# A backbone step's output projection in the shadow of a scan: transpositions in the scans' PSUM banks, input blocks split one at a time

## The chip, the core and the metric

The kernel runs on one core of a Trainium2 chip. The metric is the device time of one execution in microseconds (us), the median of several runs. The core has five engines with a queue each: TensorE (PE in the profile; its weight loads are PEld), VectorE (DVE), ScalarE (ACT), GpSimd (POOL) and SyncE (SP), which here issues nearly all transfers. Engines wait for one another through semaphores, and each takes its own instructions strictly in order. Matmuls write to PSUM, a small memory of eight banks, from which VectorE and ScalarE read.

## The reference

One layer of a hybrid backbone, for 128 context tokens and 512 latent tokens of width 2048, is computed as one batch of 640 columns:

```python
h = _rmsnorm(x, lp['norm1_g']) * (1.0 + sc1) + sh1
p = h @ lp['w_in']
o_a, s_fin = _rwkv7_bidir(shift_fn(p[..., :C_SHIFT], ...), s0, lp)   # scans, both directions, 16 heads of 64
o_b = _chunk_gmlp(jax.nn.gelu(p[..., C_SHIFT:]), lp)                 # gated MLP over chunks of 128 tokens
x = x + g1 * (jnp.concatenate([o_a, o_b], axis=-1) @ lp['w_out'])
h = _rmsnorm(x, lp['norm2_g']) * (1.0 + sc2) + sh2
ff = (silu(h @ lp['w_ffn_gate']) * (h @ lp['w_ffn_up'])) @ lp['w_ffn_down']
return x + g2 * ff, s_fin
```

Each head's scan is a recurrence over the tokens with a 64 x 64 state. Here it is done in chunks of 64 tokens: eight steps for the latent tokens and two for the context, in both directions.

## The kernel before, in words

The program goes through w_in, the scans, the rest of w_out, and the feed-forward layer. The change lies in the scans and at the seams on both sides of them (about 1060 to 1360 us of the profile).

**Precision.** A float32 matmul operand is split into a rounded high part and the rest (`hi` and `lo` for weights, `oh` and `ol` for inputs), and three matmuls replace one: hi·oh, hi·ol and lo·oh. The split of a 128 x 640 input block is a cast on ScalarE and a subtraction on VectorE.

**w_out's input** is 16 blocks `kb` of 128 rows, stored in DRAM as `d_o`: 0 to 7 from the scans (one of each pair of heads), 8 to 15 from the gated MLP, which are there before the scans begin. `o_load(kb)` loads one and splits it. Eight of them fit in SBUF, in the slots (kb + 4) % 8: blocks 8 to 11 share their slots with 0 to 3, and 12 to 15 with 4 to 7.

**The scans.** `recur(p)` is the recurrence of pair p, a generator that TensorE's order is woven from. A step has matmuls into `w_ps`, `u_ps` and `s_ps`; VectorE and ScalarE read them, and VectorE makes the next state `SN`, which the next step's `w_ps` needs. These, and `swap` at a scan's beginning and end, take turns in a ring of four PSUM banks, the pool `pws` (tag "ws"); `y_ps` has a bank of its own. A hop calls `next` twice on each pair under way; a step takes three hops, a pair begins each ten hops (`OFF`), and there are 10·7 + 29 = 99 hops. `join` (tile `pO`) and `gate` (tile `pmm`) finish a pair that has been scanned. They use the one bank of the pool `po` (tag "g"), which VectorE reads out (L1308 and L1318).

**Wide matmuls beside them.** `wout_b()` is a second generator: w_out's product with blocks 8 to 15. For q = 0 (blocks 8 to 11) and q = 1 (blocks 12 to 15) it goes through the 16 column blocks m of the output, with 24 wide matmuls each (`big`, 128 x 320; L1086 to L1088), in portions of three that cost 0.4 in the mixer's budget; a loaded block costs 1.0. In q = 0 it also loads x's columns and transposes them: `pxT` (L1343), four transpositions and then one, into the bank of `po`, from which ScalarE copies them to `x1T` (L1344). `add_out` then adds the product to x1T on VectorE. The mixer `m3` runs blocks 8 to 11 and the first FRONT = 4 column blocks before the scans. In the scans each hop gives it an equal share of what is left but for the last REST = 6 column blocks, and that comes to two portions, six wide matmuls, in most hops:

```python
                m3.run(max(0.0, m3.left - REST * 3.2) / (hops - hop))
```

**What sets the order.** TensorE's order in the scans is as written (`manual_schedule`). The other engines' order is made by a scheduler, which can move an instruction ahead of where the code has it as soon as it takes its inputs to be there. `split` (L171 to L173) is the load and the split of a block of weights.

Of the kernel before, what the change touches and what calls it, by code (L numbers as in the profile page):

```python
# [10 lines left out]
F32 = mybir.dt.float32  # L11
# [8 lines left out]
P = 128  # L20
# [38 lines left out]
FRONT = 4  # L59
# [30 lines left out]
def flow_step(ctx: ExitStack, tc, x_prompt, x_sample, state_rwkv, c, c_ctx, w_mod, b_mod,  # L90
# [18 lines left out]
    def tpool(**a):  # L109
        if a.get("space") != DRAM:  # L110
            a["reuse_waits"] = "tile"
        return tc.tile_pool(**a)
# [861 lines left out]
    g = 0  # L974
# [83 lines left out]
    pbig = obx.enter_context(tpool(name="pbig", bufs=2, space=PSUM))  # L1058
    o_hi, o_lo = {}, {}

    def o_load(kb, src=None):

        j = (kb + 4) % 8
        o_hi[kb], o_lo[kb] = (obp[j // 4].tile([P, T], F32R, tag=f"{n}{j}", name=n) for n in ("oh", "ol"))
        raw = o_lo[kb].bitcast(F32) if src is None else src
        if src is None:
            nc.sync.dma_start(raw, d_o[kb])
        S.copy(o_hi[kb], raw)
        V.tensor_sub(o_lo[kb], raw, o_hi[kb].bitcast(F32))

# [2 lines left out]
    def wout(m, q):  # L1073


        halves = [pbig.tile([P, HALF], F32, tag="big", name="big") for _ in range(2)]
        n = KB * q + m
        for k in range(n if n == 0 else n + 1, min(n + 2, 2 * KB)):
            r0, c0 = (8 + 4 * (k // KB)) * P, k % KB * P
            ahead[k] = split(w_out[0, r0:r0 + 4 * P, c0:c0 + P], 4)  # L1080
        hi, lo = ahead.pop(n)
        for hf in range(2):
            s = slice(HALF * hf, HALF * hf + HALF)
            for k in range(4):
                kb = 8 + 4 * q + k
                TE.matmul(halves[hf], hi[:, k, :], o_hi[kb][:, s], start=(k == 0), stop=False)  # L1086
                TE.matmul(halves[hf], hi[:, k, :], o_lo[kb][:, s], start=False, stop=False)
                TE.matmul(halves[hf], lo[:, k, :], o_hi[kb][:, s], start=False, stop=(k == 3))  # L1088
                yield 0.4
            add_out(m, halves, hf)  # L1090
# [11 lines left out]
    with ExitStack() as ph:  # L1102
        rw = ph.enter_context(tpool(name="rw", bufs=1))
        sm = ph.enter_context(tpool(name="sm", bufs=2))
        po = ph.enter_context(tpool(name="po", bufs=1, space=PSUM))
        pws = ph.enter_context(tpool(name="pws", bufs=4, space=PSUM))
# [21 lines left out]
        def load_next():  # L1128
            if todo:
                _, p, ctx_, step = todo.pop(0)  # L1130
                r = rw.tile([P, 2, REC], F32, tag="rec", name="rec", bufs=NREC)
                nc.sync.dma_start(r, d_S[p].rearrange("p d c f -> p (d c) f")[:, flip(seqs[ctx_][step])])
                recs[p, ctx_, step] = r
# [165 lines left out]
        def join(p, i):  # L1299

            u = U[p]
            a, b = HV[i]
            ps = po.tile([P, 5, CH], F32, tag="g", name="pO")
            for cc in range(a, b):
                for h in range(2):
                    TE.matmul(ps[hsl(h), cc - a, :], u.Y[1][hsl(h), cc, :], I2[hsl(h), :], start=True, stop=True)
            dst = v3(u.bv)[:, a:b, :]
            V.scalar_tensor_tensor(out=dst, in0=ps, scalar=prm[:, C_GW + p:C_GW + p + 1],  # L1308
                                   in1=dst, op0=ALU.mult, op1=ALU.add)
# [14 lines left out]
        def wout_b():  # L1324

            for q in range(2):
                for kb in range(8 + 4 * q, 12 + 4 * q):
                    o_load(kb)
                    yield 1.0
                for m in range(KB):  # L1330
                    if q == 0:
                        xc = x1T[m].rearrange("p (t n) -> p t n", n=P)
                        for t0, src in ((0, x_sample[0]), (NT - 1, x_prompt[0])):
                            n = src.shape[0] // P
                            nc.sync.dma_start(xc[:, t0:t0 + n, :],
                                              src[:, m * P:(m + 1) * P].rearrange("(q t) c -> t q c", t=P))
                    for k, c in enumerate(wout(m, q)):
                        yield c
                        if q == 0 and k in (0, 2):
                            t0, t1 = ((0, 4), (4, 5))[k // 2]  # L1340
                            ps = po.tile([P, 4, P], F32, tag="g", name="pxT")
                            for t in range(t0, t1):
                                TE.transpose(ps[:, t - t0, :], xc[:, t, :], ident)  # L1343
                            S.copy(xc[:, t0:t1, :], ps[:, 0:t1 - t0, :])  # L1344
# [11 lines left out]
        S.copy(gss[64:96, 2], gss[32:64, 2].bitcast(F32))  # L1356
        m3 = Mixer()
        m3.add(wout_b(), 8.0 + 16 * 6.4)
        m3.run(4.0 + FRONT * 3.2)
        for _ in range(NREC - 4):  # L1360
            load_next()
        act, nxt, after = [], 0, []
        hops = OFF * (NPAIR - 1) + 29
        with tc.manual_schedule(engines={mybir.EngineType.PE}):
            for hop in range(hops):
                if hop == OFF * nxt and nxt < NPAIR:
                    act.append((nxt, recur(nxt)))
                    nxt += 1
                for p, gen in act:
                    next(gen)  # L1370
                for job in list(after):
                    if job[0] < 0:
                        next(job[2], None)
                    elif job[0] in (LATE, LATE + 1):
                        join(job[1], job[0] - LATE)
                for p, gen in list(act):
                    if next(gen, 0) == 0:
                        act.remove((p, gen))
                        after.append([-7, p, norm(p)])
                for job in list(after):  # L1380
                    if job[0] in (LATE + 2, LATE + 3):
                        gate(job[1], job[0] - LATE - 2)
                    job[0] += 1
                    if job[0] > LATE + 3:
                        after.remove(job)
                m3.run(max(0.0, m3.left - REST * 3.2) / (hops - hop))
                for _ in range(owed[1]):
                    load_next()
                owed[:] = 0, owed[0]
                if hop == hops - 12:  # L1390
                    for kb in range(4):
                        o_load(kb)

            assert not act
            (_, p, gen), = after
            for _ in gen:
                pass
            for i, work in enumerate((lambda: join(p, 0), lambda: join(p, 1), lambda: gate(p, 0), lambda: gate(p, 1))):
                while m3.left > (4 - i) * 1.6 - 0.1:
                    m3.run(0.01)  # L1400
                work()
            m3.drain()
# [77 lines left out]
    with ExitStack() as ph:  # L1480
# [58 lines left out]
        for hf in range(2):  # L1539
            s = slice(HALF * hf, HALF * hf + HALF)  # L1540
            for m in range(KB):
                if hf or m >= AHEAD:
                    four_blocks(hf, m, 0)
                ps = four_blocks(hf, m, 1)
# [517 lines left out]
    later = []  # L2062
# [75 lines left out]
    for t in (3, 4, 0, 1, 2):  # L2138
        for h in (1, 0):
            out = fin.tile([P, 4, 256], F32, tag=f"out{h}", name="out")  # L2140
            src = acc[:, 4 * h:4 * h + 4, t * 256:(t + 1) * 256]
# [36 lines left out]
```

## Time and profile before

| | |
|---|---|
| time, median of 3 runs | 3168.68 us (3168.43 to 3176.81) |
| the profiled execution's own time | 3172.49 us |
| its span, first to last instruction | 3170.7 us |
| TensorE, VectorE, ScalarE, GpSimd busy | 96%, 74%, 47%, 39% of the span |
| the scans | about 1085 to 1325 us |

In the profile, `out<-in` names the tiles that an instruction writes and reads, L1198 its line, and xN how many. In rows in order of time the first number is the start, the second the time taken, and brackets tell how long the engine sat idle before and what ended that. In a list of waits stand the total, the number of times, and the longest. In a table of stretches each engine has its busy time and the number of its instructions; then come the granted clock of TensorE as a share of full speed, the share of time in which the transfer engines were busy, and what they moved. SPq is SyncE's queue issuing a transfer.

### The profile page before, as it was taken

Reading aid. Unit: us, or ns where it says so; the run is one execution under the profiler, and the core shown is the slowest. Engines: PE = TensorE matmul, PEld = TensorE weight load, DVE = VectorE, ACT = ScalarE, POOL = GpSimd, SP = SyncE. Lnnn points to the kernel's source line nnn. Section 1 sums busy time; section 2 is a strip of 40 time slices with the busy share of each in tenths; the row PEclk is TensorE's granted clock in tenths of the full one; section 3 lists DMA queues with packets and bytes.
Section 4 is the critical chain, followed back from the end, with each engine's and each line's share of the span. In section 5 each row is a group of like instructions: output and inputs, shape, how many; then the busy total and the mean of one; then the engine's idle time right before and its main releaser. Section 6 shows DMA issues by size and latency. Waiting matters only on the chain.

```text
span 3170.7 us, 71552 instructions
## 1 busy us (share of the span) xinstructions
PE 3052.5 (96%) x27896; PEld 2846.7 (90%) x27896; DVE 2357.5 (74%) x4119; ACT 1475.2 (47%) x3216; POOL 1235.3 (39%) x1081
## 2 busy tenths in 40 slices
PE   6999999999999998999999999999999999999997
PEld 3688878888878887899999999999999999999997
DVE  4566677667776688767877877777787788888788
ACT  3344544555444444357444444444444454444365
POOL 2001121121122034511456665666656645555542
PEclk9999999999999999999999999999999999999999
DMA  9767786777777688575343334434344365554453
GB/s 371 249 191 203 211 226 182 210 208 202 204 198 214 212 281 282 160 220 156 110 131 109 120 115 128 127 107 121 116 128 122 107 198 151 164 170 129 128 165 123
DMA packets 740435, 550.83 MB, mean 174 GB/s; under 512 B 141056, under 2 KB 673504, under 8 KB 731264
## 3 DMA queue, kind: packets, MB, share of 16 engines
q1 hardware_dynamic: 727136, 532.47, 55.6%
q0 software_dynamic: 10624, 13.23, 1.9%
q8 instruction: 219, 3.59, 0.5%
q14 instruction: 120, 0.98, 0.1%
q10 hardware_dynamic: 2336, 0.57, 0.1%
HBM read 437.79 MB, written 110.95 MB: 173 GB/s over the span
## 4 chain that ended last, share of the span: by engine, by line
PE 46%; DVE 3%; issue 1%; DMA 1%; POOL 0%; ACT 0%; DVEq 0%; POOLq 0%; ACTq 0%
PE P L1696 15%; PE P L1693 15%; PE P L1694 15%; DVE lo L1474 1%; DMA x1d<-d_x 1%; DVE xd L1762 1%; DVE cd L1941 0%; DVE out L2145 0%; DMA d_op<-act 0%; POOL rawd L1602 0%; DVE cd L1963 0%; PE P L2074 0%; DVE cd L1968 0%; DVE cd L1957 0%; POOL t L1602 0%
## 5 line engine op out<-in xcount | busy, mean ns | idle before, releaser
L1693 PE MATMUL P<-xo,hi 128*128 128x320 f32 x2352 | 700.0, 310 | 0.2 <-ACT hi L1473 0.2
L1694 PE MATMUL P<-xo,hi 128*128 128x320 f32 x2352 | 699.7, 309 | 0.0
L1474 DVE TENSOR_TENSOR lo<-raw,hi 128x512 fp32r<-128x512 f32 x526 | 512.0, 978 | 171.5 <-ACT hi L1473 169.3
L1473 ACT CAST hi<-raw 128x512 fp32r<-128x512 f32 x526 | 326.7, 622 | 467.3 <-PE P L1694 390.1
L194 PE MATMUL big<-h_hi,hi 128*128 128x320 f32 x1376 | 439.2, 326 | 8.2 <-ACT hi L172 4.9
L1696 PE MATMUL P<-xo,lo 128*128 128x320 f32 x2352 | 441.4, 310 | 3.7 <-DVE lo L1474 3.7
L1693 PEld LDWEIGHTS P<-xo,hi 128*128 128x128 f32 x2352 | 442.0, 188 | 0.6 <-ACT hi L1473 0.5
L1694 PEld LDWEIGHTS P<-xo,hi 128*128 128x128 f32 x2352 | 442.3, 188 | 0.0
L195 PE MATMUL big<-h_lo,hi 128*128 128x320 f32 x1376 | 424.5, 315 | 0.8 <-DVE h_lo L358 0.8
L1602 POOL TENSOR_TENSOR raw<-raw 128x512 f32<-128x512 f32 x252 | 411.3, 1641 | 18.2 <-DVE lo L1474 10.0
L1696 PEld LDWEIGHTS P<-xo,lo 128*128 128x128 f32 x2352 | 369.4, 188 | 4.6 <-DVE lo L1474 4.6
L1693 PE MATMUL P<-xd,hi 128*128 128x320 f32 x1232 | 367.4, 310 | 3.7 <-ACT P L2075 2.0
L1694 PE MATMUL P<-xd,hi 128*128 128x320 f32 x1232 | 366.8, 309 | 0.0
L198 PE MATMUL big<-h_hi,lo 128*128 128x320 f32 x1376 | 321.0, 314 | 2.2 <-DVE lo L173 2.0
L194 PEld LDWEIGHTS big<-h_hi,hi 128*128 128x128 f32 x1376 | 262.7, 191 | 58.1 <-issue 25.5
L173 DVE TENSOR_TENSOR lo<-raw,hi 128x512 fp32r<-128x512 f32 x268 | 186.8, 700 | 157.1 <-ACT hi L172 154.6
L1602 POOL TENSOR_TENSOR t<-raw 128x512 f32<-128x512 f32 x84 | 124.5, 1482 | 424.8 <-DMA raw<-in_w_ffn_up_dram 416.0
L1473 ACT CAST hi<-rawd 128x512 fp32r<-128x512 f32 (+1 forms) x288 | 167.3, 586 | 239.8 <-PE P L1694 159.1
L195 PEld LDWEIGHTS big<-h_lo,hi 128*128 128x128 f32 x1376 | 263.0, 191 | 5.9 <-DVE h_lo L358 1.9
L172 ACT CAST hi<-raw 128x512 fp32r<-128x512 f32 x268 | 164.5, 618 | 221.2 <-PE big L195 80.5
L1474 DVE TENSOR_TENSOR lo<-rawd,hi 128x512 fp32r<-128x512 f32 (+1 forms) x288 | 233.9, 820 | 24.5 <-ACT hi L1473 23.8
L1696 PE MATMUL P<-xd,lo 128*128 128x320 f32 x1232 | 236.4, 310 | 5.3 <-DVE lo L1474 5.3
(406 smaller groups left out, 6087.1 us busy)
## 6 DMA issues: line engine op xcount, KB each, us to landing
wt<-in_w_mod_dram SPq DMA_DIRECT2D x96, 1024.0 KB
raw<-in_w_ffn_gate_dram SPq DMA_DIRECT2D x182, 256.0 KB
raw<-in_w_ffn_up_dram SPq DMA_DIRECT2D x182, 256.0 KB
rec<-d_S SPq DMA_DIRECT2D x80, 576.0 KB
raw<-in_w_in_dram SPq DMA_DIRECT2D x172, 256.0 KB
rawd<-in_w_ffn_down_dram SPq DMA_DIRECT2D x128, 256.0 KB
raw<-in_w_out_dram SPq DMA_DIRECT2D x96, 256.0 KB
xd<-d_os SPq DMA_DIRECT2D x66, 320.0 KB
```

Of the source, the lines that this page charges most:

```text
L172: S.copy(hi, raw)
L173: V.tensor_sub(lo, raw, hi.bitcast(F32))
L194: TE.matmul(halves[hf], hi[:, k, :], h_hi[:, kb, s], start=(kb == 0), stop=False)
L195: TE.matmul(halves[hf], hi[:, k, :], h_lo[:, kb, s], start=False, stop=False)
L198: TE.matmul(halves[hf], lo[:, j - 4 * q, :], h_hi[:, j, s], start=False, stop=(j == KB - 1))
L1473: S.copy(hi[:, 0:nk], raw[:, 0:nk])
L1474: V.tensor_sub(lo[:, 0:nk], raw[:, 0:nk], hi[:, 0:nk].bitcast(F32))
L1602: G.tensor_tensor(out=o[:, 0:nk], in0=p[:, 0:nk], in1=q[:, 0:nk], op=ALU.subtract)
L1693: TE.matmul(ps, hi[:, k, :], xk[:, 0, :], start=q == 0 and k == 0 and not filled, stop=False)
L1694: TE.matmul(ps, hi[:, k, :], xk[:, 1, :], start=False, stop=False)
L1696: TE.matmul(ps, lo[:, k, :], x(i, 4 * q + k)[:, 0, :], start=False, stop=q == nq - 1 and k == nk - 1 and last)
L1762: (G if (k + q) in POOLK else V).tensor_tensor(out=x[:, 1, :], in0=t[:, q, :], in1=x[:, 0, :].bitcast(F32), op=ALU.subtract)
```

## The change

`o_load` can leave out the split, and `o_split` does it later. Blocks 12 to 15 are no longer loaded between q = 0 and q = 1. Within q = 0 each is loaded at m = 3, 6, 9 and 12, and split three column blocks later, at the same cost of 1.0. Blocks 0 to 3 were loaded and split in the hop twelve before the end; now one is loaded each four hops of the last sixteen, and split three hops after its load. Blocks 8 to 11, at w_in's end, stay as they were. From m = 4 on, pxT takes a bank of `pws` and not that of `po`.

```diff
-    def o_load(kb, src=None):
+    def o_load(kb, src=None, later=False):
...
             nc.sync.dma_start(raw, d_o[kb])
+        if not later:
+            o_split(kb, raw)
+
+    def o_split(kb, raw=None):
+
+        raw = o_lo[kb].bitcast(F32) if raw is None else raw
         S.copy(o_hi[kb], raw)
         V.tensor_sub(o_lo[kb], raw, o_hi[kb].bitcast(F32))
...
             for q in range(2):
-                for kb in range(8 + 4 * q, 12 + 4 * q):
+                for kb in range(8, 12 if q == 0 else 8):
                     o_load(kb)
                     yield 1.0
                 for m in range(KB):
+                    if q == 0 and m in (6, 9, 12, 15):
+                        o_split(10 + m // 3)
+                        yield 1.0
+                    if q == 0 and m in (3, 6, 9, 12):
+                        o_load(11 + m // 3, later=True)
...
-                            ps = po.tile([P, 4, P], F32, tag="g", name="pxT")
+                            pool, tag = (po, "g") if m < FRONT else (pws, "ws")
+                            ps = pool.tile([P, 4, P], F32, tag=tag, name="pxT")
...
-                if hop == hops - 12:
-                    for kb in range(4):
-                        o_load(kb)
+                if 1 <= hops - hop <= 16:
+                    k, r = divmod(16 - hops + hop, 4)
+                    if r == 0:
+                        o_load(k, later=True)
+                    elif r == 3:
+                        o_split(k)
```

The lines below the diff's first place move down, so that L1198 (w_ps) becomes L1204, L1218 (u_ps) L1224, L1245 (s_ps) L1251, L1086 to L1088 (big) L1092 to L1094, L1068 (the cast) L1074, L1223 (rec on ScalarE) L1229, and L1343 (pxT) L1355.

TensorE at the end of q = 0, before, from the last wide matmul on (y_ps is the scans' output):

```order
L1088 MATMUL big<-oh,lo 128x320
L1218 MATMUL u_ps<-W,rec 64x64 x4
L1198 MATMUL w_ps<-ST,rec 64x64 x4
L1245 MATMUL s_ps<-rec 64x64 x4
L1198 MATMUL w_ps<-SN,rec 64x64 x4
L1171 MATMUL y_ps<-SN,rec 64x64 x4
L1218 MATMUL u_ps<-W,rec 64x64 x4
L1218 MATMUL u_ps<-rec 64x64 x4
L1181 MATMUL y_ps<-rec 64x64 x4
L1245 MATMUL s_ps<-rec 64x64 x4
L1218 MATMUL u_ps<-W,rec 64x64 x4
L1198 MATMUL w_ps<-SN,rec 64x64 x4
```

and after, at the same two hops of the scans:

```order
L1094 MATMUL big<-oh,lo 128x320
L1224 MATMUL u_ps<-W,rec 64x64 x4
L1204 MATMUL w_ps<-ST,rec 64x64 x4
L1251 MATMUL s_ps<-rec 64x64 x4
L1204 MATMUL w_ps<-SN,rec 64x64 x4
L1177 MATMUL y_ps<-SN,rec 64x64 x4
L1224 MATMUL u_ps<-W,rec 64x64 x4
L1224 MATMUL u_ps<-rec 64x64 x4
L1187 MATMUL y_ps<-rec 64x64 x4
L1251 MATMUL s_ps<-rec 64x64 x4
L1092 MATMUL big<-oh,hi 128x320
L1093 MATMUL big<-ol,hi 128x320
```

Before, the scans' matmuls go on alone through six hops; now the wide ones come back after the first of them (here the pause for block 15). There are two such places more, at the pauses for blocks 13 and 14, each of one hop; the pause for block 12 shows as hops with half of their wide matmuls.

ScalarE, at the end of q = 0, before (`rec` and `Y` are the scans'):

```order
L1223 COPY rec<-u_ps 64x2x64
L1068 CAST oh<-ol 128x640
L1223 COPY rec<-u_ps 64x2x64
L1186 ACTIVATE Y,ys<-y_ps 128x64 x2
L1223 COPY rec<-u_ps 64x2x64 x2
L1068 CAST oh<-ol 128x640
L1186 ACTIVATE Y,ys<-y_ps 128x64 x2
L1068 CAST oh<-ol 128x640
L1223 COPY rec<-u_ps 64x2x64
L1186 ACTIVATE Y,ys<-y_ps 128x64 x4
L1068 CAST oh<-ol 128x640
```

and after, some ten hops into the scans, where block 14 stands now:

```order
L1192 ACTIVATE Y,ys<-y_ps 128x64 x2
L172 CAST hi<-raw 128x512
L1074 CAST oh<-ol 128x640
L1229 COPY rec<-u_ps 64x2x64
L1192 ACTIVATE Y,ys<-y_ps 128x64 x4
L1356 COPY x1T<-pxT 128x512
L1229 COPY rec<-u_ps 64x2x64
```

The four casts that stood together between the scans' copies stand apart, and the scheduler has put three of them much earlier than the code has them.

SyncE, at the scans' beginning, before:

```order
L171 DMA raw<-in_w_out_dram 128x4x128 x2
L1335 DMA x1T<-in_x_sample_dram 128x4x128
L1335 DMA x1T<-in_x_prompt_dram 128x128
L1132 DMA rec<-d_S 128x2x576 x2
L171 DMA raw<-in_w_out_dram 128x4x128
```

and after:

```order
L171 DMA raw<-in_w_out_dram 128x4x128 x2
L1067 DMA ol<-d_o 128x640
L1138 DMA rec<-d_S 128x2x576 x2
L1346 DMA x1T<-in_x_sample_dram 128x4x128
L1346 DMA x1T<-in_x_prompt_dram 128x128
```

The load of block 13 stands where x's load stood, and x's has moved behind two loads of the scans' records.

## The prediction

> **What bounds the kernel now.** I read the page first, then the stretches in which the changed instructions run, then what TensorE waits for there, and last the order of time around each wait.
>
> ```profile
> span 3170.7 us, 71552 instructions
> PE 3052.5 (96%) x27896; PEld 2846.7 (90%) x27896; DVE 2357.5 (74%) x4119; ACT 1475.2 (47%) x3216; POOL 1235.3 (39%) x1081
> ```
>
> TensorE is the bound: 96% of the span, and no other engine is above 74% (the weight loads, PEld, run beside it). So what the change is worth is what it does to TensorE's idle time in the scans. There I cut the stage at the last and the first wide matmul around w_out's second group of blocks:
>
> ```profile
> core 0: us, PE busy (x) PEld busy (x) DVE busy (x) ACT busy (x) POOL busy (x), PEclk, DMA share, GB/s
> 1085.00:1216.70 131.70, 127.20 (x2189) 109.39 (x2187) 100.50 (x335) 57.33 (x272) 37.79 (x48) 1.00 0.88 276
> 1216.70:1233.20 16.50, 11.90 (x301) 10.59 (x301) 13.69 (x43) 8.07 (x34) 2.11 (x5) 1.00 0.88 295
> 1233.20:1325.00 91.80, 90.82 (x1580) 77.87 (x1579) 81.00 (x252) 41.13 (x196) 49.62 (x62) 1.00 0.70 226
> sum 240.00, PE 229.93 PEld 197.86 DVE 195.19 ACT 106.53 POOL 89.52; mean PE 76.64 PEld 65.95 DVE 65.06 ACT 35.51 POOL 29.84
> ```
>
> The scans take 240 us, TensorE idles 240.00 − 229.93 = 10.07 us of them, and that is all that can be won here. It lies unevenly: 4.50 us in the first 131.7 us, 4.60 us in the 16.5 us of the turn, 0.98 us in the last 91.8 us. The granted clock is 1.00 in all three, so it plays no part. With 99 hops in about 240 us a hop lasts about 2.4 us. The waits:
>
> ```profile
> PE w_ps L1198 <- DVE SN L1253: 4.1, 7, 1.5
> PE pxT L1343 <- DVE bv L1318: 1.3, 1, 1.3
> PE y_ps L1171 <- ACT Y L1186: 1.0, 1, 1.0
> ...
> PE pxT L1343 <- DVE bv L1308: 0.5, 1, 0.5
> ```
>
> Two kinds stand out: the recurrence waiting for its new state (SN, from VectorE), and a transposition waiting for a join (L1308) or a gate (L1318) to leave the one bank that they share.
>
> **Part 1, the turn.** Before, four blocks stand between the last transposition and w_out's second half, each paying 1.0 into the mixer's budget and issuing nothing on TensorE. For about six hops no wide matmul lies between one step of a scan and the next:
>
> ```profile
> 1218.40 0.52 PE L1198 MATMUL w_ps<-SN,rec 64*64 64x64 f32 x7 [0.79 <-DVE SN L1253]
> 1221.13 0.52 PE L1198 MATMUL w_ps<-SN,rec 64*64 64x64 f32 x7 [0.52 <-DVE SN L1253]
> 1223.83 0.85 PE L1198 MATMUL w_ps<-SN,rec 64*64 64x64 f32 x15 [0.72 <-ACT oh L1068]
> 1227.14 0.45 PE L1171 MATMUL y_ps<-SN,rec 64*64 64x64 f32 x8 [1.03 <-ACT Y L1186]
> 1231.03 0.52 PE L1198 MATMUL w_ps<-SN,rec 64*64 64x64 f32 x7 [1.54 <-DVE SN L1253]
> ```
>
> 0.79 + 0.52 + 0.72 + 1.03 + 1.54 = 4.60 us, the stretch's whole idle time. After, the same 4.0 of budget is paid in four places. The wide matmuls' number and cost stay as they were, they only spread, so each microsecond of idle that they fill is won. Term: −4.60.
>
> What comes back: in the new order I count three hops left without a wide matmul, one of which holds a gate's four matmuls, which take as long as a hop's usual six wide ones:
>
> ```profile
> 1207.25 0.85 PE L1317 MATMUL pmm<-gss,gate 128*128 128x320 f32 x4
> ```
>
> Two bare hops remain, single ones. A single one costs what the turn's first two cost, 0.79 and 0.52, before the blocks' casts pile up: 2 × 0.65 = +1.3 us. The bounds are 0 (their neighbours' wide matmuls cover it) and three at 0.79, +2.4. I take 1.3, since the turn's first hop waited although wide matmuls ran right before it.
>
> **Part 2, the bank of the transpositions.** From the fifth block of columns on, pxT takes a bank of the scans' four instead of the one of joins and gates.
>
> ```profile
> 1198.39 0.33 PE L1343 MATMUL pxT<-ident,x1T 128*128 128x128 f32 x1 [0.52 <-DVE bv L1308]
> 1209.39 0.66 PE L1343 MATMUL pxT<-ident,x1T 128*128 128x128 f32 x4 [1.29 <-DVE bv L1318]
> ```
>
> These two waits, 1.81 us, lose their reason. Not all of it is won, since VectorE is behind there:
>
> ```profile
> 1208.80 0.53 DVE L1318 SCALAR_TENSOR_TENSOR bv<-bv,gb,pmm 128x320 f32<-128x320 f32 x1
> 1209.53 0.87 DVE L1287 TENSOR_REDUCE ys<-sq 128x5 f32<-128x320 f32 x2
> 1210.91 0.28 DVE L1222 COPY rec<-u_ps 64x128 f32<-64x128 f32 x1 [0.51 <-PE u_ps L1218]
> ```
>
> The next step's copy (rec) stood behind two reductions that ended at 1210.40 and waited 0.51 us more: had TensorE come earlier, the scan would have gained these 0.51 us, not 1.29. Between 0.5 and 1.81 I take half: −0.9 us.
>
> The price in the scans' ring: a pxT bank is held from its first transposition to the end of ScalarE's copy.
>
> ```profile
> 1090.81 0.60 PE L1343 MATMUL pxT<-ident,x1T 128*128 128x128 f32 x4
> 1091.45 0.59 ACT L1344 COPY x1T<-pxT 128x512 f32<-128x512 f32 x1 [4.13 <-PE pxT L1343]
> ```
>
> That is 1092.04 − 1090.81 = 1.23 us. A scan step takes about three banks a hop (w_ps, u_ps, s_ps), so with a pxT among them a bank comes round after four allocations, about a hop or 2.4 us. 1.23 is inside it: 0. What hides it is that spare 1.2 us; the upper bound is under the rivals.
>
> **Part 3, blocks that are split earlier.** The four casts and subtractions of the turn do not stay where the code has them: the scheduler pulls the first three into the first ten hops, and one of them, block 12, in front of the scans, where its load is the fifth in a row on SyncE's queue. Their work is no more than before:
>
> ```profile
> L1068 ACT CAST oh<-ol 128x640 fp32r<-128x640 f32 x8 | 5.7, 727 | 2.7 <-DMA ol<-d_o 2.7
> L1069 DVE TENSOR_TENSOR ol<-ol,oh 128x640 fp32r<-128x640 f32 x8 | 6.5, 812 | 1.3 <-ACT oh L1068 1.3
> L172 ACT CAST hi<-raw 128x512 fp32r<-128x512 f32 x23 | 14.2, 621 | 15.0 <-DMA raw<-in_w_out_dram 9.8 <-PE big L1087 3.8 <-ACT Y L1186 1.4
> ```
>
> Eight casts of 0.73 us and eight subtractions of 0.81 us move to other hops: three of each to the scans' first hops, one to their middle, four over their end. But a cast on ScalarE's queue holds the scan's copies behind it when its transfer is late, and transfers are slow here (DMA share 0.88):
>
> ```profile
> 1186.21 0.46 SPq L1335 DMA_DIRECT2D x1T<-in_x_sample_dram  x1
> ...
> 1187.27 0.43 SPq L171 DMA_DIRECT2D raw<-in_w_out_dram  x1
> ...
> 1194.15 0.62 ACT L172 CAST hi<-raw 128x512 fp32r<-128x512 f32 x1 [2.22 <-DMA raw<-in_w_out_dram]
> ...
> 1193.11 0.66 PE L1343 MATMUL pxT<-ident,x1T 128*128 128x128 f32 x4 [0.72 <-DMA x1T<-in_x_sample_dram]
> 1195.74 0.71 PE L1198 MATMUL w_ps<-SN,rec 64*64 64x64 f32 x11 [0.71 <-DVE SN L1253]
> ```
>
> 1194.15 − 1187.27 = 6.9 us from issue to use; the cast waited 2.22 us, VectorE's subtraction behind it, the new state SN behind that, and TensorE 0.71 us at w_ps. A block's cast in the same position costs the same 0.71. Before, the eight casts waited 2.7 us together; for the new places I add one such wait, rounded: +0.5 us (bounds: 0, and 8 × 0.71 = 5.7). SyncE's queue also carries the four loads ahead of x's loads; a late x cost the 0.72 us above once. In the order x's load now stands behind a block's and two records, but it goes out some three hops ahead (1186.21 for 1193.11), and of the twelve column blocks in the scans this one alone came late: 0 (bound 4 × 0.72 = 2.9).
>
> The Trainium skill, page "DMA: Bandwidth & Descriptors", section "Anatomy of one DMA — SWDGE (gpsimd) path", fits a transfer as about 2.0 us plus its bytes over 436 GB/s; for a block's 327,680 bytes that is an estimate of 2.75 us. By it the moved casts would wait for nothing and the sum below would be 0.5 us better. The trace does not agree under this load: 6.9 us for a smaller transfer of 256 KB (the fit is of another queue).
>
> **Part 4, the last four blocks.** Before, they were loaded and split in one hop, twelve before the end; now over sixteen hops. That stretch idles 0.98 us in all, and of the waits listed none in it names these blocks. Nothing to win: 0 (bounds −0.98, and the casts' price, counted in part 3). They are needed only after the scans, behind six more column blocks of wide matmuls, which hide the last split.
>
> **Sum.** −4.60 + 1.3 − 0.9 + 0.5 = −3.7 us. The profiled execution took 3172.49 us (1.8 us around its span); it becomes 3168.8. The median of the runs, 3168.68, lies 3.81 us under it; the same step gives 3165.0 us.
>
> **Rivals.** *A: the idle time only moves.* VectorE is busy 13.69 of the turn's 16.5 us and 195.19 of the scans' 240: if the chain through SN is what limits, a gap reopens at each hop with none or half of its wide matmuls. Three bare hops at 0.79 and four halved ones at 0.5 make 4.4 of the 4.60 us, and part 2 wins nothing. For it: SN is the largest wait. Against: of the 4.1 us in seven waits for SN, 0.79 + 0.52 + 1.54 + 0.71 are told above; the other three make 0.5 us in all the 80 hops outside the turn, many of which have half their wide matmuls. It gives about 3168.5.
>
> *B, the slower side: late transfers.* Blocks 12 to 15 are now loaded while x and w_out's weights load too. If each load finds the queue 7 us deep, its cast stalls ScalarE as at 1194.15 and pushes an x load as at 1193.11: 0.71 + 0.72 = 1.43 us each, 5.7 for four, and 4 × 0.71 = 2.8 for the last four. Against the 4.2 us gained without it that is +4.3: 3173. It decides from three of the first four loads on. Against it: the DMA share hardly rises, four blocks of 320 KB in 130 us are 10 GB/s on 276.
>
> *C: the ring of four.* If ScalarE copies late, the scans wait for the bank. The slowest case in the trace starts at 1193.11 and is copied at
>
> ```profile
> 1195.20 0.58 ACT L1344 COPY x1T<-pxT 128x512 f32<-128x512 f32 x1
> ```
>
> so 2.67 us, 0.3 beyond a hop. Were all 24 pxT of the scans so late, 24 × 0.3 = 7.2 us would be lost, net +3.5: 3172. It decides from a hold of 2.4 us on, in half of them; the trace has one. The Trainium skill, page "PSUM — Partial Sum Buffer", section "PSUM bank collisions raise a hardware error", has that two engines may not touch one bank and quadrant at once and that the hardware does not arbitrate, so a wait per bank is needed: this rule speaks against the change. The trace agrees that such a wait exists: pxT's 0.52 and 1.29 us.
>
> *D: all of it goes.* If the spread matmuls cover the small waits as well, up to 10.07 us: 3158.6 to 3162.
>
> **How the numbers follow.** Forecast 0.58 (its own range 3162.5 to 3167.5), A 0.20, B 0.10, C 0.06, D 0.06. The range 3161.0 to 3171.0 holds the forecast, A, and parts of B, C and D, about 0.88; I leave it there because the runs of one kernel alone reach 8 us apart (3168.43 to 3176.81). About 0.3%, 9.5 us, is what a measurement of this kernel can tell from no change. Faster by that needs nearly all of the 10.07 us, the edge of D: 0.03. Slower by that needs B with every load late and C at once: 0.04. The rest, 0.93, is within it.
>
> **What would show it.** Right: the turn's gap of 16.5 us without wide matmuls is gone and TensorE's idle time in the scans is near 6 us; pxT waits for no bv; the casts' waits on ol stay near 3 us. Part 1 is wrong if w_ps still waits over 3 us for SN; part 2 if pxT still waits, or if scan matmuls wait for x1T (rival C); part 3 if oh waits for ol by 6 us or more (rival B).

## The result, and the profile after

The changed kernel is slower: 3177.76 us (median of 16 runs) against 3172.24 us for the kernel before, run beside it. The ratio is 1.0019 (95% interval 1.0012 to 1.0026), or +6.0 us (3.8 to 8.2). The prediction was −3.7 us, a ratio of 0.9988. Below, a ratio always stands against runs of the kernel before on the same chip, and 0.001 of it is 3.2 us.

The page of the profile after, whose execution took 3177.97 us:

```profile
span 3176.2 us, 71539 instructions
PE 3055.8 (96%) x27896; PEld 2846.8 (90%) x27896; DVE 2340.3 (74%) x4119; ACT 1476.1 (46%) x3216; POOL 1236.4 (39%) x1081
```

The work is the same; the span is 5.5 us longer. The view of stretches, from w_in's last wide matmul to the last gate (pmm), first of the kernel before, then of the changed one:

```profile
1064.92:1352.35 287.43, 274.82 (x4431) 239.92 (x4430) 227.67 (x692) 125.23 (x537) 103.93 (x130) 1.00 0.77 247
```

```profile
1063.31:1356.46 293.15, 276.63 (x4431) 240.62 (x4429) 228.70 (x692) 125.71 (x538) 102.61 (x130) 0.99 0.76 241
```

This stage is 5.72 us longer, so it holds the whole loss of this execution: idle time rose from 12.61 to 16.52 us (length minus PE busy), and the same matmuls took 1.81 us more. Now the same view cut at equal places of the work, which are the first, the 328th, the 379th and the last of the 576 s_ps matmuls: before the turn, the turn, after the turn. The kernel before:

```profile
1095.00:1217.40 122.40, 118.20 (x2126) 101.30 (x2125) 95.12 (x321) 55.37 (x267) 37.79 (x48) 1.00 0.88 275
1217.40:1237.90 20.50, 15.90 (x357) 14.00 (x354) 17.68 (x58) 11.58 (x51) 6.56 (x10) 1.00 0.82 272
1237.90:1316.60 78.70, 77.72 (x1384) 66.72 (x1386) 71.44 (x223) 35.70 (x168) 41.57 (x51) 1.00 0.77 249
```

and the changed kernel:

```profile
1093.80:1213.70 119.90, 115.01 (x2097) 98.19 (x2096) 96.12 (x320) 55.88 (x267) 37.62 (x48) 1.00 0.89 283
1213.70:1236.10 22.40, 18.86 (x386) 16.38 (x382) 16.87 (x57) 10.29 (x50) 7.20 (x11) 1.00 0.87 267
1236.10:1320.70 84.60, 79.06 (x1384) 67.84 (x1384) 71.39 (x224) 36.30 (x168) 39.70 (x51) 0.98 0.71 221
```

Idle time was 4.20, 4.60 and 0.98 us; it is 4.89, 3.54 and 5.54 us. The turn lost only 1.1 us of its idle time, and the stretch after it, whose 1384 matmuls are the same, is 5.9 us longer. Of these, 4.6 us are idle time and 1.3 us slower matmuls. The wide matmuls alone (tile `big`), before and after:

```profile
1095.00:1217.40 122.40, 53.88 (x271) 1.00 0.88 275
1217.40:1237.90 20.50, 1.64 (x9) 1.00 0.82 272
```

```profile
1093.80:1213.70 119.90, 50.51 (x247) 1.00 0.89 283
1213.70:1236.10 22.40, 6.57 (x33) 1.00 0.87 267
```

24 wide matmuls went into the turn, and 24 are missing ahead of it. TensorE's waits in the changed kernel:

```profile
PE w_ps L1204 <- DVE SN L1259: 6.2, 7, 2.1
PE pxT L1355 <- DMA x1T<-in_x_sample_dram: 3.8, 3, 2.1
PE s_ps L1251 <- ACT rec L1229: 1.8, 3, 1.2
PE pxT L1355 <- ACT x1T L1356: 1.1, 2, 0.8
PE big L1094 <- DVE lo L173: 0.8, 1, 0.8
PE u_ps L1224 <- DVE W L1213: 0.7, 2, 0.5
```

pxT's waits for bv are gone. In their place stand late columns of x (3.8 us, before 0.7) and the copies to x1T (1.1 us, before 0.3), and SN costs 6.2 us where it cost 4.1. The longest wait for x, from the order of time:

```profile
1213.66 0.47 SPq L1346 DMA_DIRECT2D x1T<-in_x_sample_dram  x1
...
1219.51 0.63 PE L1355 MATMUL pxT<-ident,x1T 128*128 128x128 f32 x4 [2.10 <-DMA x1T<-in_x_sample_dram]
```

The load went out 5.9 us ahead of its use. The longest wait for SN has a late transfer behind it too:

```profile
1236.88 0.50 SPq L171 DMA_DIRECT2D raw<-in_w_out_dram  x1
...
1243.64 0.62 ACT L172 CAST hi<-raw 128x512 fp32r<-128x512 f32 x1 [2.15 <-DMA raw<-in_w_out_dram]
1244.29 0.79 DVE L173 TENSOR_TENSOR lo<-raw,hi 128x512 fp32r<-128x512 f32 x1 [1.58 <-ACT hi L172]
1245.60 0.46 DVE L1259 SCALAR_TENSOR_TENSOR SN<-s_ps,gend,SG 128x64 f32<-128x64 f32 x2
1245.93 0.54 PE L1204 MATMUL w_ps<-SN,rec 64*64 64x64 f32 x6 [2.07 <-DVE SN L1259]
```

A block of w_out's weights came 6.8 us after its issue. ScalarE's cast stood waiting for it, VectorE's subtraction behind the cast, SN behind the subtraction, and TensorE behind SN.

### The profile page after: what moved, and what is told of

Its sections match the earlier page's. It is cut to its first block, busy times and chain, and to the rows that moved or that the text cites. A ratio compares the mean times of both kernels' runs of the same rounds, so it can differ in the third digit from the quotient of the medians.

```text
span 3176.2 us, 71539 instructions
## 1 busy us (share of the span) xinstructions
PE 3055.8 (96%) x27896; PEld 2846.8 (90%) x27896; DVE 2340.3 (74%) x4119; ACT 1476.1 (46%) x3216; POOL 1236.4 (39%) x1081
## 4 chain that ended last, share of the span: by engine, by line
PE 64%; DVE 7%; DMA 3%; issue 2%; ACT 2%; POOL 0%; SPq 0%; DVEq 0%; POOLq 0%; ACTq 0%
PE P L1711 15%; PE P L1708 15%; PE P L1709 15%; PE big L194 2%; PE big L198 2%; PE big L195 2%; PE big L1092 1%; DVE lo L1489 1%; DMA raw<-in_w_out_dram 1%; PE big L1094 1%; PE big L1547 1%; PE big L1549 1%; PE big L1548 1%; PE big L1093 1%; PE y_ps L1187 1%
## 5 line engine op out<-in xcount | busy, mean ns | idle before, releaser
L1489 DVE TENSOR_TENSOR lo<-raw,hi 128x512 fp32r<-128x512 f32 x526 | 503.8, 963 | 180.1 <-ACT hi L1488 177.1
L173 DVE TENSOR_TENSOR lo<-raw,hi 128x512 fp32r<-128x512 f32 x268 | 187.1, 701 | 161.4 <-ACT hi L172 159.7
```

The costliest lines, as they stand in the source:

```text
L173: V.tensor_sub(lo, raw, hi.bitcast(F32))
L1489: V.tensor_sub(lo[:, 0:nk], raw[:, 0:nk], hi[:, 0:nk].bitcast(F32))
```

## The experiments

"x in time" means that each column block of x is loaded two column blocks earlier than it was:

```diff
+                        for mm in range(0 if m == 0 else m + 2, min(KB, m + 2 + 1)):
+                            xc = x1T[mm].rearrange("p (t n) -> p t n", n=P)
+                            for t0, src in ((0, x_sample[0]), (NT - 1, x_prompt[0])):
...
                         xc = x1T[m].rearrange("p (t n) -> p t n", n=P)
-                        for t0, src in ((0, x_sample[0]), (NT - 1, x_prompt[0])):
...
```

All results in one table. "Stage" is the time from w_in's last wide matmul to the last gate in the run's one profile, and "idle" TensorE's idle time before, in and after the turn, cut as above. One profile is one execution: over the 19 kernels measured beside the kernel before, the stage's difference from it and the difference by the ratio correlate at 0.82; the stage says 1.7 us more on average, with a scatter of 2.2 us about that, so the ratio decides. The stage also holds falls of the granted clock, which the last section counts: none in the kernel before, one in the changed one, three in bank and turn.

| kernel | ratio (95% interval) | stage, us | idle, us |
|---|---|---|---|
| before | 1 | 287.4 | 4.2, 4.6, 1.0 |
| changed | 1.0019 (1.0012 to 1.0026) | 293.2 | 4.9, 3.5, 5.5 |
| bank alone | 0.9988 (0.9979 to 0.9997) | 285.6 | 2.1, 2.8, 1.8 |
| turn alone | 1.0009 (1.0001 to 1.0018) | 291.0 | 6.5, 1.9, 3.3 |
| end alone | 0.9995 (0.9984 to 1.0006) | 288.4 | 3.3, 6.2, 1.1 |
| changed, x in time | 0.9993 (0.9984 to 1.0002) | 289.6 | 5.6, 1.9, 2.8 |
| changed, loads of 12 to 15 first | 1.0027 (1.0016 to 1.0037) | 295.0 | 5.7, 2.8, 5.3 |
| bank and turn | 1.0014 (1.0005 to 1.0023) | 297.6 | 6.0, 3.7, 3.7 |
| changed, x and weights in time | 0.9997 (0.9987 to 1.0006) | 285.3 | 1.9, 2.0, 2.0 |
| bank, x and weights in time | 0.9998 (0.9989 to 1.0006) | 291.6 | 4.7, 3.9, 3.2 |
| before, x in time | 1.0006 (0.9998 to 1.0015) | 291.5 | 6.0, 3.7, 2.7 |
| bank, x in time | 1.0003 (0.9994 to 1.0012) | 287.9 | 3.4, 4.2, 1.8 |
| turn, x in time | 1.0010 (1.0002 to 1.0019) | 294.3 | 7.2, 1.7, 5.0 |
| changed, x in time, no pauses | 0.9993 (0.9983 to 1.0003) | 284.6 | 2.9, 0.6, 1.1 |
| turn filled, no load moved | 1.0002 (0.9991 to 1.0013) | 290.6 | 7.1, 1.4, 1.5 |
| the same with the bank | 1.0008 (1.0000 to 1.0017) | 290.4 | 8.2, 1.2, 1.6 |
| bank and end | 0.9989 (0.9980 to 0.9998) | 286.6 | 1.3, 3.8, 2.9 |
| early loads, pauses left in the turn | 1.0006 (0.9997 to 1.0014) | 289.9 | 6.5, 2.8, 1.0 |
| changed, one block of weights | 0.9989 (0.9977 to 1.0001) | 282.4 | 3.7, 1.4, 2.9 |
| before, one block of weights | 0.9982 (0.9972 to 0.9992) | 286.9 | 3.9, 5.6, 1.6 |

**The parts alone.** The bank part:

```diff
-                            ps = po.tile([P, 4, P], F32, tag="g", name="pxT")
+                            pool, tag = (po, "g") if m < FRONT else (pws, "ws")
+                            ps = pool.tile([P, 4, P], F32, tag=tag, name="pxT")
```

> Only the bank: pxT from the fifth column block on goes to the scans' ring of four, blocks 12 to 15 and 0 to 3 as before. Theory T (the loss is late transfers, from loads that now stand among those of x and w_out): the bank costs nothing, ratio 0.9995 to 1.000, pxT's waits for bv (1.81 us) gone. Rival R (the ring): the scans' matmuls wait for x1T's copies, 5 us slower or more (ratio 1.0015 and up).

The turn part (the hunk of `wout_b` without the two lines of pxT's pool):

```diff
-                for kb in range(8 + 4 * q, 12 + 4 * q):
+                for kb in range(8, 12 if q == 0 else 8):
...
+                    if q == 0 and m in (6, 9, 12, 15):
+                        o_split(10 + m // 3)
+                        yield 1.0
+                    if q == 0 and m in (3, 6, 9, 12):
+                        o_load(11 + m // 3, later=True)
```

> Only the turn: blocks 12 to 15 loaded and split one at a time within q = 0, pxT in the old bank, blocks 0 to 3 as before. T: the 4.6 us of the turn are won, but x's and w_out's transfers come later (x waits near 3 us, waits for SN behind a late weight 3 us or more): +1 to +3 us, ratio 1.0003 to 1.001. R: the turn alone wins about 4 us, 0.9985 to 0.999. Rival M (splits between the steps of the scans' last hops hold up VectorE): the same as R here.

The end part:

```diff
-                if hop == hops - 12:
-                    for kb in range(4):
-                        o_load(kb)
+                if 1 <= hops - hop <= 16:
...
```

> Only the end: blocks 0 to 3 loaded and split over the last 16 hops, all else as before. T: two late weights behind them, about +2 us (1.0006). M: four splits in the scans' VectorE queue, about +4 us or more (1.0012), with the waits for SN behind L1075's subtraction and not behind a late cast. R: 0 (1.000).

The bank alone is a gain of 3.8 us (1.0 to 6.7), so rival R, that it costs, falls; it is also more than T's 0.9995 to 1.000. In its trace pxT waits for no bv, and the scans wait 1.1 us for x1T's copies:

```profile
PE w_ps L1198 <- DVE SN L1253: 2.5, 6, 0.6
PE w_ps L1198 <- ACT x1T L1345: 1.1, 2, 1.0
```

The end alone makes no difference that can be told; M's 4 us lie outside its interval. The turn alone is a loss of 2.9 us (0.3 to 5.7), inside T's 1 to 3 us. The parts add up to −2.5 us and the whole is +6.0, so they do not add.

**Bank and turn together.** The end part is left out of the changed kernel.

> The changed kernel without its end part (blocks 0 to 3 as before). If the parts add: -0.0012 + 0.0009, ratio 0.9997. If the end matters only together with the others: as 0.9997 too. If bank and turn work against each other (the turn's late x holds a bank of the ring): 1.0015 to 1.002, with waits for x at pxT of 3 us or more.

The third case came, with 1.0014 just under its 1.0015 and x waiting 5.0 us. TensorE's waits with the turn alone, and then with the bank beside it:

```profile
PE pxT L1354 <- DMA x1T<-in_x_sample_dram: 2.9, 3, 1.3
PE pxT L1354 <- DVE bv L1324: 1.3, 1, 1.3
PE pxT L1354 <- DVE bv L1314: 1.1, 2, 0.8
```

```profile
PE pxT L1355 <- DMA x1T<-in_x_sample_dram: 5.0, 3, 2.3
```

With the turn's order pxT waits 5.3 us, 2.4 of them for bv. With the bank changed too it waits 5.0 us for x and no longer for bv (ahead of the scans, at 1080 us, it also waits 2.8 us once for x1T's copy). So the bank's wait seems to have covered a part of x's lateness, and its removal to be paid back at the next wait; no run shows this apart from the rest.

**x in time.** In the changed kernel:

> The changed kernel with x's columns loaded two column blocks earlier in the code. T: x's 3.8 us of waits at pxT go, so 3 to 4 us better than the changed kernel, near 3174 (ratio to before 1.0006); w_out's late weights stay. R and M: no gain, ratio to before 1.0015 to 1.002.

In the kernel before, as a control; and with the bank part, and with the turn part alone:

> A control: the kernel before, with x's columns loaded two column blocks earlier and nothing else. Before, x came late once, by 0.72 us. T (x late is what the change costs): 0 to 1 us, ratio 0.9995 to 1.000. If loading x early is worth as much here as in the changed kernel (0.0026), the gain there was not from the change's own late x: 0.9975 to 0.998.

> The kernel before with the bank part and x two column blocks earlier. T: the bank alone, 0.9988, since x waited for nothing in it; with weights ahead as well it was 0.9998, so if weights far ahead were what hurt there, this one is near 0.9988; if x far ahead hurt, near 0.9998.

> The turn part alone with x two column blocks earlier. The turn alone was 1.0009 with 2.9 us of waits for x. Prediction's part 1 (the turn's 4.6 us are won, 1.3 come back): 0.999. Rival A (the idle time only moves to other hops): 1.000, with the waits for SN and rec outside the turn at 4 us or more.

In the changed kernel the loss is gone: from 1.0019 to 0.9993, a difference of 0.0026 ± 0.0012 or about 8 us, twice what T expected and twice the 3.8 us of waits for x. In the kernel before, loading x earlier gains nothing (1.0006), as T expected, and with the bank it costs 0.0015 ± 0.0013. So x early is no gain as such. It has a price too: in all five kernels that load x earlier and leave the weights alone, TensorE waits 1.5 us once, at the scans' beginning, for the cast of a block of weights, and the granted clock falls there. In the kernel before with x in time, for instance:

```profile
PE big L1086 <- ACT hi L172: 1.5, 1, 1.5
```

The scheduler has put this cast behind ScalarE's first Y instructions, ahead of which it stands without the early loads. But with the turn alone it is worth nothing either (1.0009 and 1.0010): x's 2.9 us are gone, and other waits have grown in that trace. For TensorE and for ScalarE:

```profile
PE w_ps L1204 <- DVE SN L1259: 8.4, 9, 1.5
```

```profile
ACT hi L172 <- DMA raw<-in_w_out_dram: 8.4, 10, 1.9
ACT gate L1279 <- DMA graw<-in_g_dram: 5.3, 5, 2.9
```

Waits for SN of 4 us or more were rival A's sign, but its ratio there was 1.000, under the interval of 1.0002 to 1.0019, and late weights and gates stand behind these waits. By the price above, 1.5 us and a fall of the clock that costs up to 1.7 us (an estimate from the last section), the 2.9 us won at x would be paid back, as they were. What that leaves unaccounted for is the changed kernel, which pays the same price and gains 8 us.

How late is late can be read from the profiles together. For the last ten column blocks of x in each of the 20 kernels (200 loads), the time from SyncE's issue to the first transposition, and whether that one waited for x (for a late load it is the time that the transfer took):

| issue to use | loads | late | longest wait, us |
|---|---|---|---|
| under 6 us | 10 | 9 | 2.3 |
| 6 to 7 us | 15 | 5 | 3.0 |
| over 7 us | 175 | 0 | |

The kernel before had its last three loads at 6.4, 6.9 and 9.7 us, one of them late. The changed kernel has its last four at 6.2, 5.0, 6.6 and 5.9 us, three of them late. With x in time the changed kernel has none under 20 us.

**The blocks' loads out of x's way.**

```diff
+                for kb in range(12, 16 if q == 0 else 12):
+                    o_load(kb, later=True)
...
-                    if q == 0 and m in (3, 6, 9, 12):
-                        o_load(11 + m // 3, later=True)
```

> The changed kernel, with blocks 12 to 15 loaded right behind 8 to 11, ahead of x's columns, and still split one at a time where the changed kernel splits them. If the blocks' loads among x's are what makes x late: pxT's 3.8 us of waits for x fall under 1 us, ratio to before about 1.0010. Rival P (the pauses move the column blocks against x's loads, whatever else is loaded): waits for x stay at 3 us or more, ratio 1.0015 to 1.002.

The ratio is 1.0027, and x still waits 2.6 us, with leads of 5.4 and 4.9 us. So it is not the blocks' loads beside x's that make x late. Rival P is what is left, that the pauses move the column blocks against SyncE's queue, but nothing here changes that alone. The ratio is above P's own 1.0015 to 1.002, and the granted clock has a part in it: its mean over the runs is 0.988, and 0.991 over those of the kernel before beside them.

**The turn without moved loads.** Blocks 12 to 15 stay where they were and cost nothing in the budget:

```diff
                     o_load(kb)
-                    yield 1.0
+                    if q == 0:
+                        yield 1.0
...
-        m3.add(wout_b(), 8.0 + 16 * 6.4)
+        m3.add(wout_b(), 4.0 + 16 * 6.4)
```

> The kernel before, in which blocks 12 to 15 are loaded and split at the same place but cost nothing in the mixer's budget: wide matmuls go on through the turn, and nothing else moves. If the turn's idle time is due to missing wide matmuls alone (prediction's part 1): its 4.6 us fall under 1.5 us, ratio 0.9988. If the four casts between the scans' copies, or a late transfer, hold the turn: waits for SN, oh or lo of 3 us or more stay there, ratio 0.9995 to 1.001.

> The same with the bank part. Alone the bank was 0.9988. If both add: 0.9976 to 0.998. If pxT, which no longer waits for bv, then waits for x or its copy instead, as in the changed kernel: no better than 0.9988.

The stretches of the first of the two:

```profile
1089.50:1216.00 126.50, 119.45 (x2110) 101.42 (x2109) 92.47 (x319) 55.11 (x266) 37.40 (x48) 0.99 0.87 266
1216.00:1236.90 20.90, 19.55 (x383) 16.62 (x381) 18.23 (x60) 11.55 (x52) 3.98 (x8) 1.00 0.85 278
1236.90:1314.80 77.90, 76.41 (x1377) 65.51 (x1375) 68.76 (x221) 36.56 (x170) 43.86 (x53) 1.00 0.77 245
```

The turn's idle time falls from 4.60 to 1.35 us. It has 27 wide matmuls more, 15 of them from the stretch before it, whose idle time rises from 4.20 to 7.05 us. The largest wait there is now pxT's for the bank of joins and gates, 3.8 us where it was 1.8; SN's rises from 0.9 to 2.0 us:

```profile
PE pxT L1344 <- DVE bv L1318: 3.8, 3, 1.9
```

The time does not move (1.0002). The idle time went under 1.5 us as expected of missing wide matmuls, and the gain expected with it did not come. With the bank the ratio is 1.0008, no gain either, and TensorE's longest wait of all for x is there:

```profile
1212.13 0.59 SPq L1336 DMA_DIRECT2D x1T<-in_x_sample_dram  x1
...
1218.35 0.87 PE L1345 MATMUL pxT<-ident,x1T 128*128 128x128 f32 x3 [3.00 <-DMA x1T<-in_x_sample_dram]
```

**Loads early, pauses in the turn**, and the bank with the end:

```diff
-                for kb in range(8 + 4 * q, 12 + 4 * q):
+                for kb in range(8, 12 if q == 0 else 8):
...
+                for kb in range(12, 16 if q == 1 else 12):
+                    o_split(kb)
+                    yield 1.0
                 for m in range(KB):
+                    if q == 0 and m in (3, 6, 9, 12):
+                        o_load(11 + m // 3, later=True)
```

> The turn part with the loads of blocks 12 to 15 spread over q = 0 as in it, but the pauses left where they were, four together between q = 0 and q = 1. The turn part alone was 1.0009. If the early loads and their early casts are what costs: x waits 2 us or more, casts of weights wait as before, the turn's hole stays, ratio 1.0015 or more. If the spread pauses cost (column blocks that come late against their loads): x waits under 1 us, ratio 0.9995 to 1.0005.

> Bank and end without the turn. If the turn's loads are the part that turns the sum over: 0.9983 (0.9988 and 0.9995 together), x waiting for nothing. If bank and end work against each other: 1.000 or above.

The first, 1.0006, lies next to the second case (0.9995 to 1.0005), and its interval ends at 1.0014, just short of the first. x waited 0.4 us there, as the second case had it. But the turn part with its pauses had 1.0009, which cannot be told from 1.0006: whether early loads or spread pauses make the turn's loss stays open. The second is 0.9989: without the turn the bank keeps its gain. It and the bank alone are the best of the kernels that do the whole work, and both beat the kernel before as well as the changed one.

**No pauses.** x in time, and the splits cost no budget, by leaving out the `yield 1.0` behind `o_split`, with the same total as above:

> The changed kernel with x two column blocks earlier, in which the split of a block in the scans costs nothing in the mixer's budget, so that no hop goes without wide matmuls for it. With the pauses it was 0.9993. If the bare hops cost what the prediction took (1.3 us): 0.9989. If they are covered: 0.9993.

```profile
1093.30:1214.10 120.80, 117.90 (x2108) 101.15 (x2109) 94.54 (x321) 56.22 (x268) 38.40 (x48) 0.99 0.88 282
1214.10:1233.80 19.70, 19.14 (x385) 16.67 (x384) 16.80 (x58) 9.12 (x45) 4.21 (x8) 1.00 0.85 264
1233.80:1311.40 77.60, 76.47 (x1377) 65.36 (x1375) 69.81 (x221) 37.08 (x175) 42.45 (x53) 1.00 0.76 246
```

Its ratio is that of the kernel with pauses. In the trace the idle time is 4.6 us (2.90, 0.56 and 1.13) against 9.8 before, the picture that the prediction had of the change, and the wide matmuls stand in the turn as in the kernel with the turn filled. By its interval the ratio is 0.9983 to 1.0003, which holds both cases and no change too.

**Weights.** The weights two column blocks ahead:

```diff
-        for k in range(n if n == 0 else n + 1, min(n + 2, 2 * KB)):
+        for k in range(n if n == 0 else n + 2, min(n + 3, 2 * KB)):
```

> The changed kernel with x's columns two column blocks earlier, and w_out's weights two column blocks ahead of their use where it was one. T: the casts of weights wait for no transfer (9.6 us of ScalarE's waits in the changed kernel fall under 2 us) and the waits for SN behind them go: 2 to 3 us better than with x alone, ratio to before 0.998 to 0.9987. Rival V (VectorE's and ScalarE's work itself is too dense, not its inputs late): as with x alone, 0.999 to 1.000.

> The kernel before with the bank part, and x and the weights two column blocks ahead; the turn and the end as before. T: the bank's -0.0012, and 1 to 2 us for late casts: ratio 0.998 to 0.9986, with the turn's waits (some 3 us) left. Rival V: 0.9988 as the bank alone.

ScalarE's waits for weights fell from 9.6 to 1.7 us in the changed kernel, as T said, and the waits for blocks grew from 1.0 to 4.9 us:

```profile
ACT oh L1074 <- DMA ol<-d_o: 4.9, 5, 2.1
...
ACT hi L172 <- DMA raw<-in_w_out_dram: 1.7, 2, 1.0
```

The ratios, 0.9997 and 0.9998, cannot be told from 0.9993 and 1.0003 with x alone: T's further 2 to 3 us did not come. The second also misses V's 0.9988.

Last, one block of weights for all column blocks, in both kernels. They leave out the other 31 blocks, and so do not compute the product:

```diff
-            ahead[k] = split(w_out[0, r0:r0 + 4 * P, c0:c0 + P], 4)
+            if not raw0:
+                raw0.append(st.tile([P, 4, P], F32, tag="raw", name="raw"))
+                nc.sync.dma_start(raw0[0], w_out[0, r0:r0 + 4 * P, c0:c0 + P].rearrange("(k p) n -> p k n", p=P))
+            whi, wlo = (st.tile([P, 4, P], F32R, tag=g, name=g) for g in ("hi", "lo"))
+            S.copy(whi, raw0[0])
+            V.tensor_sub(wlo, raw0[0], whi.bitcast(F32))
+            ahead[k] = whi, wlo
```

> The changed kernel, in which w_out's product with blocks 8 to 15 takes one block of weights for all its column blocks: it is loaded once and cast and subtracted each time, so that 31 transfers of 256 KB (7.9 of the stage's 62 MB) fall away and no cast of weights waits for one; the work of the engines stays. If late transfers are what turned the change into a loss (T): x waits under 1 us, waits for SN under 3 us, and it gains what the prediction summed over the same reduction of the kernel before: 3 to 4 us, its ratio 0.001 below that one's. If ScalarE and VectorE are the limit (V): no faster than that one.

> The kernel before with the same reduction (one block of weights for all column blocks of w_out's product with blocks 8 to 15, loaded once, cast and subtracted each time). T: the turn's waits stay (3 to 4.6 us) and most others go: ratio 0.998 to 0.999. V: as the kernel before, 0.9995 to 1.000.

The kernel before is faster by 5.7 us (2.5 to 8.9), so the transfers of weights, or what stands behind them in SyncE's queue, do cost it time; the changed one is faster by 3.5 us (−0.3 to 7.3). Between the two the change costs 0.0007 ± 0.0016 by the runs. T's gain of 0.001 lies just outside that, V's zero lies inside, and so does a loss of 6 us (0.0019). T's other sign missed too: x waits for nothing, but the waits for SN are 4.1 us, over the 3 us expected. The two profiles differ the other way, by 4.5 us (282.4 against 286.9), which says little: the changed kernel's is of its fastest execution, the other of its slowest.

## Why the prediction was wrong

**Part 3 failed at late x.** It set x's lateness at 0 with a bound of 2.9 us, because x "goes out some three hops ahead". The trace has 3.8 us, beyond the bound, and with x in time the changed kernel's 1.0019 becomes 0.9993, about 8 us, while the kernel before gains nothing from it. So the late loads are what the sum lacked; their waits are 3.8 us of the 8, and the rest is not accounted for. The row that the prediction quoted had the warning: 6.9 us of lead and 0.72 us late, so that margin was already gone before the change. The twelve loads were not alike: the first nine went out over 13 us ahead, and only the last three stood at the edge. The changed kernel has the last four there. The blocks' own casts, the term of +0.5 us, were no trouble: they wait for ol 1.0 us in all, before 2.7.

**Part 1 failed in that what is filled was not won.** It took the wide matmuls as cover that the turn gets for nothing: "they only spread, so each microsecond of idle that they fill is won". Inside the turn its sum was near: 1.3 us were to come back, and of the 3.54 us there 2.10 are late x, which leaves 1.4. But the turn alone filled its hole (4.60 to 1.91 us idle) and had 2.3 us more idle time before it and 2.3 us more after it; the filled turn without any moved load did the same (4.60 to 1.35, and 4.20 to 7.05 before it). For the turn part the prediction had −4.60 + 1.3 + 0.5 = −2.8 us; alone it measured +2.9 (0.3 to 5.7). This looks like rival A, at 0.20, but A's mechanism, a gap at SN in each hop that lost its cover, is not shown. Before the turn, the turn alone waits 2.3 us for x, 2.4 us for bv and 0.5 us for SN. And in the changed kernel with x in time and no pauses, as many wide matmuls stand in the turn, 36, as when it is filled without a moved load, and the idle time before it is 2.90 us, not 7.05. What the turn part costs beside its late x stays open.

**Part 2 was right in kind and too small**: −0.9 us expected, −3.8 (−6.7 to −1.0) alone; the ring cost 1.1 us of waits in that trace, where it had 0. But beside the turn it wins nothing that shows; there pxT waits for a late x. **Part 4** was 0 and measured −1.6 us (−5.1 to 1.9), which does not speak against it. **The clock** was to play no part, since the kernel before has 1.00 throughout; the changed kernel's profile has one fall, and 1.3 us of slower matmuls.

**The sum** added its terms as if none changed another. Alone the three parts measure −3.8, +2.9 and −1.6 us, together +6.0. The x half of rival B (whose 3173 was worked out as +4.3 us, with a chance of 0.10) came true. Of the signs that the prediction named against itself, two came: pxT still waits, for x, and w_ps waits over 3 us for SN (6.2 us); this one was weak, since it was 4.1 us before.

**Shown:** the loss lies in the scans; only loads of x with less than 7 us of lead come late; with x in time the changed kernel's loss is gone; the bank alone is a gain; the turn alone and the filled turn are none. **Seen in traces only:** idle time that leaves the turn comes back before and after it; late weights and gates stall ScalarE's queue and so SN. **Open:** why x in time is worth 8 us in the changed kernel, and whether the turn's loss is from early loads or from the pauses.

## What to carry to other kernels

The mixer spreads a fixed number of matmuls, so what fills one hole leaves another place: a term "won" needs the place from which its filler comes, and the waits that stand there. Before a wait is removed, look at what is next in line and with what margin; here a transfer with 6 to 7 us of lead under a load of 0.88 was the next wait. Try the parts of such a change alone: one was a gain, and the sum a loss.

## What the runs showed of the hardware that was not expected

The 14 loads of x that TensorE waited for came 4.8 to 6.9 us after their issue, for 256 KB each, in stretches with a transfer share of 0.78 to 0.90. With one block of weights, an eighth of the stage's bytes less, the share before the turn was still 0.86 (changed) and 0.84 (before). The Trainium skill, page "DMA: Bandwidth & Descriptors", section "Anatomy of one DMA — SWDGE (gpsimd) path", gives about 2.0 us plus the bytes over 436 GB/s, an estimate of 2.6 us for such a load. The fit is of another queue; the measurement decides, and under this load it is about twice to nearly three times that.

In the changed kernel's profile the granted clock fell right at the 2.07 us wait for SN:

```profile
1243.00:1248.00 5.00, 2.93 (x44) 2.55 (x45) 2.79 (x9) 0.88 (x2) 1.53 (x2) 0.82 0.72 246
1248.00:1253.00 5.00, 5.00 (x104) 4.31 (x102) 3.47 (x15) 2.74 (x13) 0.00 (x0) 0.84 0.59 156
```

That goes with the 1.3 us of slower matmuls after the turn. The 2.10 us wait for x at 1219.51 did not do so: the turn's clock was 1.00. The 20 profiles together say more. From w_in's last wide matmul to the last gate they have 17 falls, each to half the clock, 16 of them for 3.41 us and one for 6.83, and each begins 1.9 to 4.2 us after the beginning of a TensorE wait of 1.53 to 3.00 us. Of the 13 waits of 1.75 us or more, 12 have a fall; of the 15 waits of 1.5 to 1.7 us, five; the shorter ones have none. What decides between them is not shown. By these figures a fall of 3.41 us costs up to 1.7 us, an estimate, on top of the wait.
